# Second conv matrix ahead of the pool matrix, with seven block products for eight in half of its columns

## The chip, the cores and the metric

The kernel runs on one core of a Trainium2 chip. TensorE (PE) does the matrix products, VectorE (DVE) and ScalarE (ACT) work on vectors, GpSimd (POOL) and SyncE (SP) here mostly issue transfers from the chip's memory (HBM). Each engine works through its own queue of instructions in order and waits on semaphores for the others. The metric is the time of one execution on the device in microseconds (us), lower is better.

## The reference

One layer of a hybrid decoder in 32-bit floats: 256 tokens behind 16 learned ones, width 2048. What matters here is the middle of it:

```python
proj = u @ w_in[l]
z_pool, v_conv, g_conv, gate_a, gate_b = jnp.split(proj, splits, axis=-1)
y_a = causal_multiscale_pool(z_pool, w_pool_grp[l], pool_scale[l]) @ w_pool_out[l]
y_b = conformer_conv(v_conv, g_conv, w_dw[l], b_dw[l],
                     conv_ln_g[l], conv_ln_b[l]) @ w_conv_out[l]
m = jax.nn.sigmoid(gate_a) * y_a + jax.nn.sigmoid(gate_b) * y_b
h = h + rms_norm(m @ w_o[l], g_post_mix[l])
```

`conformer_conv` ends in a LayerNorm over 1024 channels and a swish; the result, here called s_act (256 x 1024), goes through the second conv matrix w_conv_out (1024 x 2048). The pooled branch is a small matrix per group of channels (w_pool_grp), then w_pool_out (1024 x 2048). An up and a down matrix of width 8192 follow behind w_o.

## The kernel before

**Split numbers.** Every matrix product is made from three: each 32-bit operand is split into a high part (a cast to the format that PE multiplies at full rate) and a low part (what is left), and PE adds high x high, high x low and low x high. Weights come in chunks of 1 MB, 128 x 2048 floats on chip. SP loads a chunk into one of three raw buffers, ACT casts the high part (line 276), DVE subtracts to get the low part (line 279), PE multiplies. High and low parts have three slots each, so the cast of chunk n waits until PE has done with chunk n - 3, and a raw buffer comes free when its low part is made.

**Order.** The order of each queue is written out by the program (`tc.manual_schedule()`). A list `stream` (lines 206 to 233) names the chunks in the order of their use; `fetch` (line 296) opens and splits the chunks up to two ahead of the one that it hands to PE, and then flushes the list `late` of waiting ACT work. `project_t` (line 844) is the loop of the stages here: per chunk a fetch, then 12 matmuls for each of two halves of 128 tokens (line 839), each 128x512 out; after the last chunk of a block of 512 columns, an evacuation. A list `pending` holds the small steps of the pooling and of the conv branch; `drain` issues them between blocks of matmuls, as many as a credit of microseconds (`fill`) allows, and a FETCH entry lets the rest wait for the next fetch. The LayerNorm's steps are such items: sums by PE (cs_m, cs_v), a root on ACT, a reciprocal chain on DVE (L448 to L452, `ln_newton`), the normalising product (L809), 16 activations on ACT in a row (`affine`, L814 and L815), the swish product (L820), and the split of s_act (L823, L826). Later parts of the kernel (the w_o, up and down matrices) use `Plan` (line 23), which takes work items with an engine, a cost, what they read and write, and sets their order: PE's and SP's items as written, DVE's and ACT's by when they can begin and when they are due.

**The stages around the change.** Eight gate projections of 2048 x 512 columns (b = 0: gate_a, b = 1: gate_b; `acc_gate`, four chunks each; a sigmoid into `sg[b]`), the pooled groups (`acc_grp`, one chunk w_grp, 48 matmuls of 128x256, L493), the pool matrix (`acc_po`, four blocks of two chunks; L904 multiplies the result by the gate in place), the conv matrix (`acc_co`, likewise; L953 multiplies by the second gate, L954 adds the two branches, and PE transposes the merged block, `mt`), and w_o (`o_c` and others). When the conv matrix begins, POOL's queue starts `early_sums` (line 918): four loads of 1 MB, two of them adding onto what is there, into the room of an activation that is then free. Rooms are shared by tag: "um" and "ux" hold u, the input of the gates, and after it m and `pairs_room`.

**Seven for eight.** The w_o, up and down stages already multiply in blocks by Strassen's way: a 2 x 2 block product with seven products of sums of blocks in place of eight. `sums_of_m` (line 967) makes four such sums of the activations:

```python
a11, a12, a21, a22 = (A[:, t, h] for t in range(2) for h in range(2))
nc.vector.tensor_sub(a11, a11, a21)
nc.vector.tensor_sub(a21, a21, a22)
nc.vector.scalar_tensor_tensor(a22, a11, -1.0, a22, op0=ALU.mult, op1=ALU.subtract)
nc.vector.tensor_add(a12, a12, a22)
```

## Time and profile before

| | |
|---|---|
| median of three runs | 1184.01 us (1183.78, 1184.01, 1185.14) |
| the profiled execution | 1184.03 us, span 1182.3 us |
| gates, last one ends | 327.85 us |
| pooled groups | 327.85 to 333.60 us |
| pool matrix | 333.60 to 377.15 us |
| conv matrix, with transposes | 377.15 to 423.37 us |
| mean granted TensorE clock | 0.998 of full speed |

Times in the trace count from the start of the span. In a row such as `L279 DVE TENSOR_TENSOR lo<-raw,hi 128x2048 ... x16 | 36.6, 2290 | 22.8 <-ACT hi` the line and engine come first, then what is written from what, how often, busy us and mean ns of one, then the engine's idle time just before these instructions and what ended it. In a timeline row the first number is the start, the second the duration. In the rows of the stretches each engine's busy us are followed by its count of instructions, then the granted clock, the busy share of the DMA engines and GB/s.

### The profile page before, as it was taken

The numbers are of one execution on the slowest core, as the hardware profiler recorded it, in microseconds if no ns is written. First come the engines' busy times: TensorE is split into PE (matmuls) and PEld (weight loads), VectorE is DVE, ScalarE is ACT, GpSimd is POOL, SyncE is SP. The second block draws the span as 40 slices with busy tenths as digits, with TensorE's granted clock in tenths as the row PEclk, the third lists the DMA queues.
The fourth block names the chain that finished last, engine by engine and source line by source line (L and its number), as shares of the span: only waits on it lengthen the run. The fifth ranks groups of instructions, "written<-read, shape, count | busy, mean of one in ns | idle before, by whom it ended". The sixth has DMA issues, their size and how long they took to land.

```text
span 1182.3 us, 15772 instructions
## 1 busy us (share of the span) xinstructions
PE 1172.6 (99%) x6351; PEld 1019.5 (86%) x6351; DVE 1012.0 (86%) x1095; ACT 679.9 (58%) x690; POOL 45.0 (4%) x51
## 2 busy tenths in 40 slices
PE   9999999999999999999999999999999999999997
PEld 9999988888888888898888888888888888888886
DVE  6899989986665799988998988989989989889865
ACT  6543344445754466756566766666756667666642
POOL 1000000000000001000001001000000010010000
PEclk9999999999999999999999999999999999999999
DMA  8655565555566967859869899898998998998861
GB/s 295 213 179 179 181 199 190 192 200 181 181 209 227 271 214 219 288 167 323 242 220 241 233 292 231 233 291 226 282 293 213 274 275 228 281 240 239 303 215 72
DMA packets 177883, 272.91 MB, mean 231 GB/s; under 512 B 4658, under 2 KB 92914, under 8 KB 176913
## 3 DMA queue, kind: packets, MB, share of 16 engines
q1 hardware_dynamic: 160176, 235.88, 59.2%
q0 software_dynamic: 16736, 34.76, 16.1%
q10 hardware_dynamic: 896, 1.25, 0.3%
q8 instruction: 50, 0.82, 0.3%
q14 instruction: 25, 0.20, 0.0%
HBM read 267.68 MB, written 4.19 MB: 230 GB/s over the span
## 4 chain that ended last, share of the span: by engine, by line
PE 99%; DVE 0%; DVEq 0%; issue 0%; ACT 0%; ACTq 0%
PE bank_u L498 18%; PE acc_gate L839 15%; PE bank_a L1802 10%; PE bank_u L504 9%; PE acc_up L1802 8%; PE bank_b L1802 7%; PE o_c L1185 6%; PE acc_z L493 4%; PE acc_co L839 4%; PE acc_po L839 4%; PE acc_v L493 3%; PE acc_g L493 3%; PE acc_vg L493 2%; PE acc_up L498 1%; PE bank_u L1802 1%; PE o_b L1185 1%
## 5 line engine op out<-in xcount | busy, mean ns | idle before, releaser
L498 PE MATMUL bank_u<-m,hi 128*128 128x512 f32 x960 | 328.8, 389 | 0.0
L504 PE MATMUL bank_u<-m,lo 128*128 128x256 f32 x960 | 265.2, 276 | 0.0
L276 ACT CAST hi<-raw 128x2048 fp32r<-128x2048 f32 (+2 forms) x94 | 151.1, 1620 | 187.8 <-PE acc_gate L839 37.6
L279 DVE TENSOR_TENSOR lo<-raw,hi 128x2048 fp32r<-128x2048 f32 (+2 forms) x94 | 179.8, 1924 | 60.4 <-ACT hi L276 60.1
L498 PEld LDWEIGHTS bank_u<-m,hi 128*128 128x128 f32 x960 | 180.2, 188 | 37.7
L1585 DVE TENSOR_TENSOR lo<-raw_m,hi 128x2048 fp32r<-128x2048 f32 x70 | 160.2, 2288 | 31.2 <-ACT hi L1581 31.1
L504 PEld LDWEIGHTS bank_u<-m,lo 128*128 128x128 f32 x960 | 180.2, 188 | 1.4
L1581 ACT CAST hi<-raw_m 128x2048 fp32r<-128x2048 f32 x70 | 133.9, 1913 | 74.5 <-DVE raw_m L1598 21.3
L839 PE MATMUL acc_gate<-hi,u_um 128*128 128x512 f32 x416 | 131.0, 389 | 0.0
L559 DVE SCALAR_TENSOR_TENSOR c<-a,taps,c 128x256 f32<-128x256 f32 x240 | 98.3, 473 | 0.1
L1802 PE MATMUL bank_a<-hi,forms 128*128 128x512 f32 (+1 forms) x288 | 93.5, 386 | 0.0
L839 PEld LDWEIGHTS acc_gate<-hi,u_um 128*128 128x128 f32 x416 | 78.1, 188 | 16.1
L839 PE MATMUL acc_gate<-lo,u_um 128*128 128x512 f32 x208 | 80.9, 389 | 0.0
L1585 DVE TENSOR_TENSOR lo<-raw_a,hi 128x2048 fp32r<-128x2048 f32 x29 | 66.3, 2287 | 10.8 <-ACT hi L1581 10.7
L1581 ACT CAST hi<-raw_a 128x2048 fp32r<-128x2048 f32 x29 | 55.4, 1910 | 33.8 <-PE bank_u L498 12.3
L1581 ACT CAST hi<-raw_c 128x2048 fp32r<-128x2048 f32 x27 | 51.5, 1909 | 27.2 <-PE bank_u L498 12.2
L1585 DVE TENSOR_TENSOR lo<-raw_c,hi 128x2048 fp32r<-128x2048 f32 x27 | 61.7, 2287 | 5.7 <-ACT hi L1581 5.7
L1802 PEld LDWEIGHTS bank_a<-hi,forms 128*128 128x128 f32 x288 | 53.9, 188 | 11.0
L1585 DVE TENSOR_TENSOR fourth_pair<-raw_m,fourth_pair 128x2048 fp32r<-128x2048 f32 x26 | 59.4, 2286 | 4.4 <-ACT fourth_pair L1581 4.4
L1665 ACT COPY half<-bank_u 128x256 f32<-128x256 f32 x60 | 22.2, 370 | 65.6 <-PE bank_u L504 65.6
L1802 PE MATMUL acc_up<-hi,forms 128*128 128x512 f32 x176 | 57.5, 390 | 0.0
L1802 PE MATMUL bank_a<-lo,forms 128*128 128x512 f32 (+1 forms) x144 | 55.6, 386 | 0.0
(419 smaller groups left out, 2266.9 us busy)
## 6 DMA issues: line engine op xcount, KB each, us to landing
raw<-in_w_in_dram SPq DMA_DIRECT2D x52, 1024.0 KB, 5.0
raw_m<-in_w_down_dram SPq DMA_DIRECT2D x38, 1024.0 KB, 7.1
raw_m<-in_w_down_dram POOLq DMA_DIRECT2D x22, 1024.0 KB, 10.5
raw_a<-in_w_up_dram SPq DMA_DIRECT2D x20, 1024.0 KB, 6.5
raw_c<-in_w_up_dram SPq DMA_DIRECT2D x19, 1024.0 KB, 6.4
raw_m<-in_w_up_dram SPq DMA_DIRECT2D x19, 1024.0 KB, 6.7
raw_a<-in_w_down_dram SPq DMA_DIRECT2D x13, 1024.0 KB, 7.3
raw_c<-in_w_down_dram SPq DMA_DIRECT2D x13, 1024.0 KB, 7.4
```

The lines of the kernel that those rows point to most:

```text
L276: nc.scalar.copy(hi[:, sl, cs], raw[:, sl, cs])
L279: nc.vector.tensor_sub(lo[:, sl, cs], raw[:, sl, cs], f32(hi[:, sl, cs]))
L493: nc.tensor.matmul(acc, w[:, k[0], cs], act[:, k[1], a, off:], start=first and n == 0, stop=last and n == 2)
L498: nc.tensor.matmul(acc.rearrange("p (a t) -> p a t", a=2)[:, :, ts], hi[:, k[0], cs], act[:, k[1], :, off + ts.start:off + ts.stop], start ...
L504: nc.tensor.matmul(acc[:, :T], lo[:, k[0], cs], act[:, k[1], 0, off:], start=False, stop=stop, skip_group_check=True)
L559: nc.vector.scalar_tensor_tensor(c, conv["a"][:, q, i:i + T], taps[:, q, i:i + 1], c, op0=ALU.mult, op1=ALU.add)
L839: nc.tensor.matmul(acc, act(kk)[:, a_, ts_], w_[:, k, :], start=kk == 0 and n == 0, stop=kk == nk - 1 and n == 2)
L1185: nc.tensor.matmul(acc, form(k, a_), box[w_][:, k, :], start=start and k == 0 and n == 0, stop=stop and k == CK - 1 and n == 2, skip_group ...
L1581: nc.scalar.copy(box["hi"], raw)
L1585: nc.vector.tensor_sub(box["lo"], raw, f32(box["hi"]))
L1665: nc.scalar.copy(box[j], accs[j][:, :T])
L1802: nc.tensor.matmul(acc, forms[h][:, f, k, a_, :], box[w_][:, k, cs], start=start and k == 0 and n == 0, stop=stop and k == KH - 1 and n == ...
```

## The change

The pool and the conv matrix change places: the conv matrix is now multiplied straight after the last gate, and the pool matrix comes behind it. For that the LayerNorm's steps are issued one to three chunks earlier, and the pooled groups stand ahead of the last gate, so that their chunk w_grp is ahead of the last gate's four chunks.

The conv matrix has 4 x 2 blocks of weights (512 columns by half of the 1024 channels). Column blocks 2 and 3 are multiplied as before (X20, X21, X30, X31, each for the two halves a and b of the tokens: 8 products of 12 matmuls). Column blocks 0 and 1, with two halves of channels and two halves of tokens, are made from seven products (named 1 to 7, in the order 1 5 2 6 7 3 4) in place of eight. Their four weight blocks are loaded once, into the room of u ("um"), and four of the seven operands are sums made there on DVE, in place, 128x2048 each; all operands are split as chunks are. Four sums of s_act's blocks (`conv_sums`) and their splits (`conv_forms`) are made as well. Products share three PSUM banks; ACT copies a bank to `pairs` where a partial sum is wanted later (`keep`), and DVE joins them (`joined`). The conv stage's work is given to a `Plan`, with the splits of the first two chunks of the pool matrix in it. Each finished block is multiplied by its gate in place (`gate_conv`, eight products of 128x512), and the merge of the two branches moves to the pool matrix (`evac_merged`).

Three places of the queues show it. The first is ACT's queue at the LayerNorm's 16 activations (`sq` and `c`). Before, the two casts ahead and the one behind are of chunks of the last two gates (`hi_2905` is the third chunk of the last gate):

```order
L276 CAST hi_2825<-raw_2824 128x2048
L276 CAST hi_2857<-raw_2856 128x2048
L814 ACTIVATE sq<-c,vecs 128x256
L815 ACTIVATE c<-c,vecs 128x256
...
L815 ACTIVATE c<-c,vecs 128x256
L276 CAST hi_2905<-raw_2904 128x2048
L868 ACTIVATE sg_2459<-acc_gate_0_2745,r_in 128x512
L868 ACTIVATE sg_2459<-acc_gate_1_2746,r_in 128x512
L276 CAST hi_2939<-raw_2938 128x2048
```

Now:

```order
L283 CAST hi_2760<-raw_2759 128x2048
L283 CAST hi_2797<-raw_2796 128x2048
L821 ACTIVATE sq<-c,vecs 128x256
L822 ACTIVATE c<-c,vecs 128x256
...
L822 ACTIVATE c<-c,vecs 128x256
L283 CAST hi_2845<-raw_2844 128x2048
L283 CAST hi_2875<-raw_2874 128x2048
L877 ACTIVATE sg_2459<-acc_gate_0_2757,r_in 128x512
L877 ACTIVATE sg_2459<-acc_gate_1_2758,r_in 128x512
L283 CAST hi_2908<-raw_2907 128x2048
```

The cast behind the activations (`hi_2845`) is now that of the pooled groups' weights, which PE uses ahead of the last gate.

The second is DVE's queue at the border between the two matrices. Before, `lo_3310` is the low part of the first chunk of the conv matrix, and the products around it write the gated pool blocks:

```order
L904 TENSOR_TENSOR sg_1856<-acc_po_0_3242,sg_1856 128x512
L904 TENSOR_TENSOR sg_1856<-acc_po_1_3243,sg_1856 128x512
L279 TENSOR_TENSOR lo_3310<-raw_3308,hi_3309 128x2048
L279 TENSOR_TENSOR lo_3340<-raw_3338,hi_3339 128x2048
L904 TENSOR_TENSOR sg_1856<-acc_po_0_3306,sg_1856 128x512
L904 TENSOR_TENSOR sg_1856<-acc_po_1_3307,sg_1856 128x512
L279 TENSOR_TENSOR lo_3384<-raw_3382,hi_3383 128x2048
L279 TENSOR_TENSOR lo_3414<-raw_3412,hi_3413 128x2048
L953 TENSOR_TENSOR mts<-acc_co_0_3380,sg_2459 128x512
L954 TENSOR_TENSOR mts<-mts,sg_1856 128x512
```

Now, at the end of the conv stage, with `lo_3347` the low part of the last product's weights, `lo_3385` and `lo_3389` those of the pool matrix's first two chunks:

```order
L1009 TENSOR_TENSOR lo_3347<-conv_blocks,hi_3343 128x2048
L1040 TENSOR_TENSOR sg_2459<-pairs,sg_2459 128x512
L1040 TENSOR_TENSOR sg_2459<-acc_ca_3134,sg_2459 128x512
L1040 TENSOR_TENSOR sg_2459<-acc_cb_3151,sg_2459 128x512
L1040 TENSOR_TENSOR sg_2459<-acc_ca_3196,sg_2459 128x512
L1040 TENSOR_TENSOR sg_2459<-acc_cb_3214,sg_2459 128x512
L1045 TENSOR_TENSOR pairs<-pairs 128x512
L1040 TENSOR_TENSOR sg_2459<-pairs,sg_2459 128x512
L1009 TENSOR_TENSOR lo_3385<-raw_c_3209,hi_3361 128x2048
L1045 TENSOR_TENSOR pairs<-acc_co_3128,pairs 128x512
L1040 TENSOR_TENSOR sg_2459<-pairs,sg_2459 128x512
L1009 TENSOR_TENSOR lo_3389<-raw_c_3229,hi_3367 128x2048
```

The first low part of the following matrix stood right behind a product on the block two before; it now stands behind a join, five gate products, another join and its gate product.

The third is SP's queue. Before, one load of a chunk after another:

```order
L271 DMA raw_3244<-in_w_pool_out_dram 128x4x512
L271 DMA raw_3274<-in_w_pool_out_dram 128x4x512
L271 DMA raw_3308<-in_w_conv_out_dram 128x4x512
L271 DMA raw_3338<-in_w_conv_out_dram 128x4x512
L271 DMA raw_3382<-in_w_conv_out_dram 128x4x512
L271 DMA raw_3412<-in_w_conv_out_dram 128x4x512
L271 DMA raw_3448<-in_w_conv_out_dram 128x4x512
L271 DMA raw_3494<-in_w_conv_out_dram 128x4x512
```

Now, from the first chunk of the conv matrix on:

```order
L278 DMA raw_3052<-in_w_conv_out_dram 128x4x512
L278 DMA raw_3091<-in_w_conv_out_dram 128x4x512
L981 DMA raw_c_3129<-in_w_conv_out_dram 128x4x512
L981 DMA raw_c_3131<-in_w_conv_out_dram 128x4x512
L985 DMA conv_blocks<-in_w_conv_out_dram 128x4x512 x4
L981 DMA raw_c_3209<-in_w_pool_out_dram 128x4x512
L981 DMA raw_c_3229<-in_w_pool_out_dram 128x4x512
L278 DMA raw_3402<-in_w_pool_out_dram 128x4x512
```

The four loads into `conv_blocks` stand in a row, and the loads of the pool matrix's first chunks (`raw_c_3209`, `raw_c_3229`, `raw_3402`) are queued behind them.

The diff, cut to its core:

```diff
+        if n == 2 * D // CW - 1:
+            stream.append((w_grp.rearrange("g (k p) c -> p (g k) c", p=P), (NG * GD // P, GD)))
         stream += columns(w_in, 0, KD, G0 + n * CW)
-    stream.append((w_grp.rearrange("g (k p) c -> p (g k) c", p=P), (NG * GD // P, GD)))
-    for w, nk in ((w_pool_out, KP), (w_conv_out, KC)):
-        for n in range(NB):
-            stream += columns(w, 0, nk, n * CW)
+
+    def conv_block(kb, n):
+        return columns(w_conv_out, kb * CK, CK, n * CW)[0]
+
+    UNITS = "X20a X20b X21a X21b X30a X30b 1 5 2 6 X31a X31b 7 3 4".split()
+    CONV = list(dict.fromkeys(u_.rstrip("ab") for u_ in UNITS))
+    stream += [conv_block(int(key[2]), int(key[1])) for key in CONV[:2]]
+    for n in range(NB):
+        stream += columns(w_pool_out, 0, KP, n * CW)
...
-    def project_t(act, nk, evac, name, fill=0.0):
+    def project_t(act, nk, evac, name, fill=0.0, often=False):
...
+                if often and t:
+                    flush()
...
-    for b in range(2):
-        sg[b] = big.tile([P, NT, D], F32, tag=f"s{b}", name=f"sg{b}")
-        for n in range(NB):
-            project_t(u_of, KD, evac_gate(b, n), f"gate{b}{n}", fill=2.9)
-
-
-    y = big.tile([P, KP, 2, T], F32R, tag="k8", bufs=2, name="y")
-    hi, lo = fetch()
-    for g in range(NG):
-        for j in range(GK):
-            q = g * GK + j
-            acc = (acc_tile if q < KP - 2 else misc_tile)(f"acc_grp_{q}")[:, :T]
-            for k in range(GK):
-                mm3(acc, hi, lo, d, (g * GK + k, g * GK + k), slice(j * P, (j + 1) * P),
-                    k == 0, k == GK - 1)
-            nc.scalar.activation(y[:, q, 0, :], acc, AF.Copy, scale=col("pool_scale", q))
-            nc.vector.scalar_tensor_tensor(y[:, q, 1, :], acc, col("pool_scale", q),
-                                           f32(y[:, q, 0, :]), op0=ALU.mult, op1=ALU.subtract)
-    drain(2.0)
...
-        pending[0:0] = [FETCH, a_[2], b_[2]]
-    pending += [(0, ln_out), (0, ln_act)]
...
-    def evac_pool(n):
-        def f(t, acc):
-            nc.vector.tensor_mul(sg[0][:, t, block(n)], acc, sg[0][:, t, block(n)])
-        return f
+        pending[0:0] = [FETCH, a_[2], b_[2], (2.4, conv_sums), FETCH] + [
+            (0.6, conv_low(key)) for key in "56"]
+    FORM_C = {"5": (0, (1, 0)), "6": (1, (1, 1)), "7": (0, (0, 0)), "3": (1, (0, 1))}
+    Sc = []
+
+    def conv_a(t, h):
+        return conv["c"][:, h * CK:(h + 1) * CK, t * P:(t + 1) * P]
+
+    def conv_sums():
+        a11, a12, a21, a22 = (conv_a(t, h) for t in range(2) for h in range(2))
+        nc.vector.tensor_sub(a11, a11, a21)
+        nc.vector.tensor_sub(a21, a21, a22)
+        nc.vector.scalar_tensor_tensor(a22, a11, -1.0, a22, op0=ALU.mult, op1=ALU.subtract)
+        nc.vector.tensor_add(a12, a12, a22)
+        Sc.append(big.tile([P, 2, CK, 2, P], F32R, tag="a", name="conv_forms"))
+        late.extend(conv_high(key) for key in "56")
+
+    def conv_high(key):
+        f, at_ = FORM_C[key]
+        return lambda: nc.scalar.copy(Sc[0][:, f, :, 0, :], conv_a(*at_))
+
+    def conv_low(key):
+        f, at_ = FORM_C[key]
+        return lambda: nc.vector.tensor_sub(Sc[0][:, f, :, 1, :], conv_a(*at_),
+                                            f32(Sc[0][:, f, :, 0, :]))
+
+    def pooled_groups():
...
+    for b in range(2):
+        sg[b] = big.tile([P, NT, D], F32, tag=f"s{b}", name=f"sg{b}")
+        for n in range(NB):
+            if (b, n) == (1, NB - 1):
+                y = pooled_groups()
+                pending += [(0, ln_out), (0, ln_act)]
+            project_t(u_of, KD, evac_gate(b, n), f"gate{b}{n}", fill=2.9, often=b)
...
-        project_t(y_of, KP, evac_pool(n), f"po{n}", fill=2.4)
...
+    blocks_room = big.tile([P, 4, CK * CW], F32, tag="um", name="conv_blocks")
+    ROOM_C = {"1": 0, "5": 0, "6": 0, "4": 0, "7": 1, "3": 2, "2": 3}
+    BLOCK_C = ((0, 0), (0, 1), (1, 1), (1, 0))
+    SUM_C = {"5": (0, 1), "6": (0, 2), "4": (0, 3), "7": (1, 2)}
+    conv_banks = {"ch": misc_tile("acc_co_chain"), "w2": misc_tile("acc_co_2"),
+                  "w3": acc_tile("acc_co_3")}
+    BANK_C = {"1": "ch", "6": "ch", "7": "ch", "4": "ch", "2": "w2", "5": "w3", "3": "w3"}
...
+    def load_block(i):
+        cplan.add("SP", 3.1, lambda: nc.sync.dma_start(
+            blocks_room[:, i].rearrange("p (k c) -> p k c", k=CK), conv_block(*BLOCK_C[i])[0]),
+            writes=(f"block{i}",), late=3.0)
...
+        name = f"block{ROOM_C[key]}" if key in ROOM_C else of_load[e]
+        if key in SUM_C:
+            to, more = SUM_C[key]
+            cplan.add("DVE", 2.22, lambda: nc.vector.tensor_add(
+                blocks_room[:, to], blocks_room[:, to], blocks_room[:, more]),
+                reads=(f"block{more}",), writes=(f"block{to}",))
+
+        def high():
+            box["hi"] = part_tile("hi", n)
+            nc.scalar.copy(box["hi"], room())
+
+        def low():
+            box["lo"] = part_tile("lo", n)
+            nc.vector.tensor_sub(box["lo"], room(), f32(box["hi"]))
+            conv_parts[e] = tuple(box[h].rearrange("p (k c) -> p k c", k=CK) for h in HALVES)
+        cplan.add("ACT", 1.83, high, reads=(name,), writes=(f"hi{q}",))
+        cplan.add("DVE", 2.22, low, reads=(name, f"hi{q}"), writes=(f"lo{q}",))
...
+    def keep(n, t, bank):
+        cplan.add("ACT", 0.5, lambda: nc.scalar.copy(h_room(n, t), conv_banks[bank]),
+                  reads=(bank,), writes=(h_of(n, t),))
+
+    def gate_conv(n, t, bank=None):
+        cplan.add("DVE", 0.62, lambda: nc.vector.tensor_mul(
+            sg[1][:, t, block(n)], conv_banks[bank] if bank else h_room(n, t),
+            sg[1][:, t, block(n)]), reads=(bank or h_of(n, t),))
+
+    def joined(n, t, op, a_, b_, names):
+        cplan.add("DVE", 0.62, lambda: op(h_room(n, t), a_(), b_()), reads=names,
+                  writes=(h_of(n, t),))
+        gate_conv(n, t)
...
+    load_c(*wanted_c.pop(0), ahead=True)
+    load_c(*wanted_c.pop(0), ahead=True)
+    for i in range(4):
+        load_block(i)
+    load_c(*wanted_c.pop(0))
+    split_done = 2
+    begun_c = set()
+    for u_, unit in enumerate(UNITS):
+        e = entry_of[unit.rstrip("ab")]
+        while split_done < len(CONV) + 2 and used.get(split_done - 3, -1) < u_ and split_done <= e + 3:
+            split_c(split_done, CONV[split_done] if split_done < len(CONV) else "pool")
+            if split_done in of_load and wanted_c:
+                load_c(*wanted_c.pop(0))
+            split_done += 1
...
+            for k in range(CK):
+                for n, (a_, w_) in enumerate(((0, hi), (0, lo), (1, hi))):
+                    nc.tensor.matmul(conv_banks[bank], form(k, a_), w_[:, k, :],
+                                     start=start and k == 0 and n == 0,
+                                     stop=k == CK - 1 and n == 2, skip_group_check=True)
+        q = slot_c(e)
+        cplan.add("PE", 2.72, product, reads=[f"hi{q}", f"lo{q}"] + (
+            [f"S{FORM_C[unit][0]}"] if unit in FORM_C else []), writes=(bank,))
+        if unit == "1":
+            keep(0, 0, "ch")
+        elif unit == "5":
+            keep(0, 1, "w3")
+            form_parts("7")
+        elif unit == "6":
+            keep(1, 0, "ch")
+            form_parts("3")
+        elif unit == "2":
+            joined(0, 0, nc.vector.tensor_add, lambda: conv_banks["w2"], lambda: h_room(0, 0),
+                   ("w2", h_of(0, 0)))
+        elif unit == "7":
+            keep(1, 1, "ch")
+            joined(1, 1, nc.vector.tensor_sub, lambda: h_room(0, 1), lambda: h_room(1, 1),
+                   (h_of(0, 1), h_of(1, 1)))
+        elif unit == "3":
+            joined(1, 0, nc.vector.tensor_sub, lambda: conv_banks["w3"], lambda: h_room(1, 0),
+                   ("w3", h_of(1, 0)))
+        elif unit == "4":
+            gate_conv(0, 1, "ch")
+        elif kb:
+            gate_conv(int(unit[1]), "ab".index(unit[3]), bank)
...
+    cplan.emit()
+    for e in ahead_p:
+        opened.append((*conv_parts[e], [], flats[e]))
...
-    def evac_conv(n):
+    def evac_merged(n):
         def f(t, acc):
             mt = mt_of(n, t)
-            nc.vector.tensor_mul(mt, acc, sg[1][:, t, block(n)])
-            nc.vector.tensor_add(mt, mt, sg[0][:, t, block(n)])
+            nc.vector.tensor_mul(mt, acc, sg[0][:, t, block(n)])
+            nc.vector.tensor_add(mt, mt, sg[1][:, t, block(n)])
...
-        project_t(s_act_of, KC, evac_conv(n), f"co{n}")
+        project_t(y_of, KP, evac_merged(n), f"po{n}")
```

More of the change, by code (lines that the diff above doesn't have):

```diff
@@ L918, in hybrid_block @@
+    while split_done < len(CONV) + 2:
+        split_c(split_done, "pool")
+        split_done += 1
+    assert not wanted_c
+    cplan.emit()
+    for e in ahead_p:
+        opened.append((*conv_parts[e], [], flats[e]))
+    at["parts"] = first_c + len(CONV) + 2
+    at["n"] += 2
     early_sums = big.tile([P, 2, CK * CW], F32, tag="k8", bufs=2, name="early_sums")
@@ L1037, in hybrid_block @@
     plan = Plan()
-    HALVES = ("hi", "lo")
     SA1, SA2, SA3, SA4 = ((1, 0), (1, 1), (0, 0), (0, 1))
```

79 lines of the change are left out of this document (75 added, 4 removed).

## The prediction

> **What bounds the kernel now.** I read the page's first part and the list of waits, then the chain of waits around the change, then busy time by stage.
>
> ```profile
> PE 1172.6 (99%) x6351; PEld 1019.5 (86%) x6351; DVE 1012.0 (86%) x1095; ACT 679.9 (58%) x690; POOL 45.0 (4%) x51
> PE idle L394 <- DVE rb L308: 1.1, 1, 1.1
> 289.50 0.24 PE cs_v L480 x2
> 289.74 38.11 PE acc_gate L839 x168
> 327.85 5.75 PE acc_grp L493 x48
> 333.60 43.55 PE acc_po L839 x192
> 377.15 16.33 PE acc_co L839 x72
> ...
> 423.37 2.73 PE o_c L1185 x12
> core 0: us, PE busy (x) PEld busy (x) DVE busy (x) ACT busy (x) POOL busy (x), PEclk, DMA share, GB/s
> 333.50:377.00 43.50, 43.50 (x194) 36.01 (x194) 26.65 (x22) 19.05 (x14) 0.00 (x0) 1.00 0.57 192
> 377.00:423.20 46.20, 46.20 (x217) 38.53 (x216) 33.55 (x32) 20.58 (x18) 4.16 (x4) 1.00 0.83 251
> ```
>
> PE waits once in the whole run, for 1.1 us, and in all stages that the change touches it is the chain: gates to 327.85, pooled groups to 333.60, pool matrix to 377.15, conv matrix to 423.37. So a matmul that is taken away is a gain, and any wait that appears on PE is a full loss. A 128x512 matmul costs 43.55 / 192 = 0.2268 us, a block of 24 (one chunk of weights) 5.44 us, a product of 12 2.72 us. DVE has room on average: 26.65 of 43.5 us in the pool stage, 33.55 of 46.2 in the conv stage. The question is whether that room stands where the new DVE work falls.
>
> The prices of the work that feeds PE, from the same two stages:
>
> ```profile
> L279 DVE TENSOR_TENSOR lo<-raw,hi 128x2048 fp32r<-128x2048 f32 x16 | 36.6, 2290 | 22.8 <-ACT hi L276 22.8
> L276 ACT CAST hi<-raw 128x2048 fp32r<-128x2048 f32 x16 | 30.6, 1914 | 32.5 <-PE acc_po L839 24.5 <-PE acc_co L839 7.1 <-DMA raw<-in_w_conv_out_dram 0.9
> 341.05 2.29 DVE L279 TENSOR_TENSOR lo<-raw,hi 128x2048 fp32r<-128x2048 f32 x1 [2.81 <-ACT hi L276]
> 343.26 0.68 DVE L904 TENSOR_TENSOR sg<-acc_po,sg 128x512 f32<-128x512 f32 x1
> 343.86 1.22 DVE L826 TENSOR_TENSOR s_act<-c,s_act 128x1024 fp32r<-128x1024 f32 x1
> 377.19 1.91 ACT L276 CAST hi<-raw 128x2048 fp32r<-128x2048 f32 x1 [2.01 <-PE acc_po L839]
> 379.13 2.29 DVE L279 TENSOR_TENSOR lo<-raw,hi 128x2048 fp32r<-128x2048 f32 x1 [1.25 <-ACT hi L276]
> ```
>
> Back to back on DVE a 128x2048 operation advances the queue by 343.26 - 341.05 = 2.21 us, a 128x512 one by 0.60. The high part starts 0.04 us after the PE block that frees its slot (377.15 to 377.19), the low part 1.94 us after that.
>
> **The change, part by part.** *Products.* Columns 0 and 1 of the conv matrix take seven products in place of eight: 192 - 180 = 12 matmuls fewer, -2.72 us. That is all the change can gain, 0.23% of the run; against it stand waits.
>
> *Order of the LayerNorm.* The conv matrix needs s_act first, so its chain runs one to three chunks earlier. The two matmuls of cs_v stand two chunks earlier on PE, behind a DVE subtraction that had slack of a chunk; I take 0.2 us of waiting (0 to 0.5).
>
> ```profile
> 293.73 1.75 DVE L448 RECIPROCAL ln_r<-ln_q 128x256 f32<-128x256 f32 x1
> 297.24 2.29 DVE L279 TENSOR_TENSOR lo<-raw,hi 128x2048 fp32r<-128x2048 f32 x1
> 299.45 2.35 DVE L809 TENSOR_TENSOR c<-c,ln_r 128x1024 f32<-128x1024 f32 x2
> 285.96 1.26 ACT L868 ACTIVATE sg<-acc_gate,r_in 128x512 f32<-128x512 f32 x2
> 302.55 0.59 ACT L814 ACTIVATE sq<-c,vecs 128x256 f32<-128x256 f32 x1
> ...
> 311.57 1.89 ACT L276 CAST hi<-raw 128x2048 fp32r<-128x2048 f32 x1
> 313.49 2.29 DVE L279 TENSOR_TENSOR lo<-raw,hi 128x2048 fp32r<-128x2048 f32 x1 [8.53 <-ACT hi L276]
> ```
>
> *The block of 16 LayerNorm activations.* It holds ACT for 311.57 - 302.55 = 9.02 us, and a weight cast stands behind it. Before, that cast ends in a low part at 313.49 + 2.29 = 315.78, while PE wants it about 316.97 + 0.23 (327.85 less two blocks, plus a matmul): 1.4 us to spare. After, the cast behind it is that of the pooled groups. Its time, on the old clock: the block boundary at 284.06 (327.85 less eight blocks and cs_v's 0.24), two sigmoids first (1.26), the cast from 285.24, its low part from 287.18 to 289.39, the reciprocal chain (297.24 - 293.73 = 3.51) to 292.90, half of the normalising product to 294.2, the activations to 303.22, the cast of the pooled groups' weights, their low part from 305.16 to 307.45. PE wants it after the seventh gate at 327.85 - 21.78 = 306.07, at its third matmul, 0.24 later, and 0.1 to 0.2 more for the wait at cs_v. The wait is about 1.1 us (0.5 to 1.6). What is queued behind on ACT is the next cast, which has a block of slack.
>
> *The conv stage on DVE.* Let T0 be its first matmul. Part slots are three, so the cast for product "1" starts when the second column block ends: T0 + 5.44 + 0.04, its low part at T0 + 7.42. From there to the end of the low part of the first pool chunk the DVE queue holds 9 low parts, the 4 weight sums and 10 operations of 128x512 (two forms, two joins, six gate products): 13 x 2.21 + 10 x 0.60 = 34.7. To that come some 0.5 for operations that read the result just ahead of them and some 0.8 for waits on products not yet ended: 36.1, so T0 + 43.5. PE ends its fifteen products at T0 + 40.8 and wants that low part one matmul later, at T0 + 41.03: a wait of 2.5 us. The least is 34.7 without any wait, 1.1 us; the most I put at 3.5, twice the extras. Before, a conv or pool chunk's low part stands two chunks ahead of its use; here six gate products and two joins, whose results no one wants soon, stand ahead of it. Inside the stage the other low parts are in time by my walk, product "2" with 0.5 us, "5" with 2.3; the last product may wait 0.3 for a copy on ACT, which shortens the later wait by as much. ACT casts 11 chunks where it cast 8 and copies four banks: some 25 us of 41, hidden.
>
> *Four weight blocks.* They load into u's room, which PE frees nine matmuls (2.0 us) ahead of T0, so with a short issue about T0 - 1.9. The nearest rows are the burst that ends in the up matrix:
>
> ```profile
> 521.52 0.37 SPq L271 DMA_DIRECT2D raw<-in_w_up_dram  x1
> ...
> 524.94 5.22 SPq L1537 DMA_DIRECT2D raw_m<-in_w_down_dram  x2
> raw<-in_w_up_dram SPq DMA_DIRECT2D x1, 1024.0 KB, 6.1
> ...
> raw_m<-in_w_down_dram SPq DMA_DIRECT2D x1, 1024.0 KB, 11.7
> ```
>
> Four loads issued from 521.52 to 524.94 land from 527.6 to 536.6: the first after 6.1 us, the others 3.0 apart. So the blocks land at T0 + 4.2, 7.2, 10.2, 13.2. They are wanted at 5.5, 9.9, 12.3 and 16.5: nothing, with 1.3 to 3.3 us of cover. If that cover goes, the whole DVE queue shifts.
>
> *The pool stage's loads.* A raw buffer comes free with its low part, so a late first chunk makes the loads late. Let P be the stage's first matmul. The raw loads for its fourth to sixth chunk are issued at about P + 2.5, P + 6 and P + 8.8; before, the loads of the last stage were issued one per block, at 370.6, 376.0 and 381.4 against its start at 377.15 (first line below: four from 376.01 on), so 9.0, 7.1 and 4.5 us earlier. The four early_sums loads on POOL's queue start at P as they did before, two of them accumulating.
>
> ```profile
> 376.01 16.69 SPq L271 DMA_DIRECT2D raw<-in_w_conv_out_dram  x4
> raw<-in_w_in_dram SPq DMA_DIRECT2D x52, 1024.0 KB, 5.0
> raw<-in_w_conv_out_dram SPq DMA_DIRECT2D x4, 1024.0 KB, 10.9
> early_sums<-in_w_o_dram POOLq DMA_DIRECT2D x4, 1024.0 KB, 11.7
> raw<-in_w_conv_out_dram SPq DMA_DIRECT2D x1, 1024.0 KB, 8.3
> q1 hardware_dynamic: 528, 1.05, 39.3%
> 400.40 1.92 ACT L276 CAST hi<-raw 128x2048 fp32r<-128x2048 f32 x1 [0.88 <-DMA raw<-in_w_conv_out_dram]
> ```
>
> The next four lines are issues with median time to landing: 5.0 us commonly, 10.9 beside early_sums, 8.3 for the load that starts just into them. The sixth line is SP's queue (q1) from 394 to 402, while the sums accumulate: 1.05 MB in 8 us. The last shows that a cast already waited for such a load. So the three land at P + 10.8, + 18.8 and + 26.8 by these rows, a microsecond later if the first shares more; cast and low part of the sixth chunk then end at P + 31.1 to 32.6 with little queued ahead, and PE wants it at 2.5 + 0.2 + 5 x 5.44 + 2 x 0.87 (two groups of transposes) = P + 31.6. I take 0.8 us (0 to 2.5). [...]
>
> *The rest.* Eight gate products move from the pool stage into the conv stage and the final merge has the two operations it had; counted above or unchanged. The w_o weights that wait for the gates' room come one DVE operation (0.7 us) later, against about 1 us of slack there: nothing.
>
> Sum: -2.72 + 0.2 + 1.1 + 2.5 + 0.8 = +1.9 us. The profiled execution took 1184.03 us (span 1182.3), the median is 1184.01, so the sum goes on the median: 1185.9.
>
> **Rivals.**
> (a) *DVE keeps up in the conv stage; not slower.* The first pool chunk's low part is ready by T0 + 41.0. For that DVE must do its 36.1 us of queue in 33.6, or start 2.5 earlier. For it: PE and ACT were never late here before. Against it: 34.7 us is bare work at back-to-back prices, and the slot rule sets the start. Sum 1183.4.
> (b) *No wait anywhere.* Then 1184.0 - 2.7 = 1181.3. It needs (a) and a LayerNorm chain more than a microsecond quicker.
> (c) *Loads late.* The four blocks share the queues' time and land together near T0 + 13, as 11.7 us for the last suggests; product "1" then starts over 7 us late, or the pool stage's loads each land one block later than I took: 1188 to 1193. Against it: loads in the burst landed in order, 3 us apart.
> (d) *The clock falls in the longest wait.* The granted clock is 1.00 in every row above and no wait of PE exceeds 1.1 us, so nothing shows what a wait of 2.5 us does; if 3.4 us of matmuls ran at half clock after it, 1.7 us more: 1187.6. [...]
>
> **How the numbers follow.** Forecast as summed, terms between their bounds (1184.8 to 1188): 0.57. (a) 0.14, (b) 0.06, (c) 0.15, (d) 0.08. About 0.2% (2.4 us) is what a measurement of this kernel can tell from no change; the lines are 1181.6 and 1186.4. Faster is (b), 0.06. Same is (a) and half of the forecast's own, 0.42. Slower is the rest, 0.52. The range leaves out (b) and the upper part of (c): 1182.8 to 1189.8.
>
> **What would show it.** Waits of PE for DVE's low part: at the pooled groups about 1 us, at the second matmul of the pool matrix 2 to 2.5, and a smaller one late in the pool stage, with a DMA behind its cast. DVE near full from T0 + 7.4 to T0 + 43.5. Blocks landing 3 us apart. If PE's waits in the conv stage itself are above 1 us, my walk of that stage is wrong; if DVE sits idle there for ACT or DMA, the loads or casts were mispriced.

## The result, and the profile after

The changed kernel takes 1189.9 us in the median of six runs (1189.2 to 1191.0) against 1183.9 before: 1.0049 of the time, 95% interval 1.0036 to 1.0062. It is slower by 6.0 us. Its profiled execution took 1189.37 us with a span of 1187.7, 5.4 us more than the profiled one of before; the shares below add up to these 5.4.

The page's first part:

```profile
PE 1173.8 (99%) x6339; PEld 1018.4 (86%) x6339; DVE 1034.4 (87%) x1113; ACT 690.0 (58%) x701; POOL 45.0 (4%) x51
```

The list of PE's waits (us in total, times, longest), which had one entry before:

```profile
PE acc_po L846 <- DVE lo L1009: 2.1, 1, 2.1
PE idle L401 <- DVE rb L315: 1.1, 1, 1.1
PE acc_grp L500 <- DVE lo L286: 0.9, 1, 0.9
PE mt L1140 <- ACT m L1144: 0.7, 1, 0.7
PE mt L1140 <- DVE mts L1159: 0.3, 1, 0.3
PE acc_co_chain L1086 <- ACT pairs L1036: 0.2, 1, 0.2
```

Four waits are new that cost more than a matmul each, and with the small one on ACT they come to 4.2 us. But PE has also become busier, 1173.8 us against 1172.6, with 12 matmuls less. Matmuls must have taken longer somewhere. The chain of waits of the changed kernel gives the stages (start and length in us):

```profile
278.69 0.44 PE cs_v L487 x2
...
303.19 1.91 ACT hi L283
305.12 2.30 DVE lo L286
307.46 5.76 PE acc_grp L500 x46
...
335.01 2.72 PE acc_ca L1086 x12
```

The conv stage begins at 335.01, where the pool stage began at 333.60 before: 1.41 later. Of that 0.07 stand already at the start of the rows (269.85 for 269.78), 0.20 in the row of cs_v, and the other 1.14 at the pooled groups, where the chain runs through the cast at 303.19 and its low part. The lengths of the two matrix stages come from PE's timeline, where a row starts some 0.16 us ahead of the chain's:

```profile
334.85 0.39 PE L1086 MATMUL acc_ca<-hi,s_act 128*128 128x512 f32 x1
...
373.25 0.50 PE L1086 MATMUL acc_co_chain<-hi,s_act 128*128 128x512 f32 x1 [0.15 <-ACT pairs L1036]
...
376.10 0.39 PE L846 MATMUL acc_po<-hi,y 128*128 128x512 f32 x1
...
428.06 0.39 PE L1385 MATMUL o_c<-hi,m 128*128 128x512 f32 x1
```

The conv stage takes 41.25 us (334.85 to 376.10) for 180 matmuls of 40.82: 0.43 lost, all at the last product, which waits for a copy on ACT. The pool stage takes 51.96 us (376.10 to 428.06); the corresponding stage before took 423.37 - 377.15 = 46.22. So the pool stage alone lost 5.74 us. Busy time by stretch, in columns as before, shows that the clock was not at full speed all through:

```profile
375.60:379.01 3.41, 1.35 (x6) 0.80 (x6) 3.41 (x3) 1.90 (x1) 1.56 (x2) 1.00 0.27 22
379.01:382.43 3.42, 3.42 (x10) 2.64 (x9) 3.38 (x4) 0.00 (x0) 0.00 (x0) 0.50 0.91 369
```

PE's timeline behind the first matmul of the pool matrix:

```profile
378.55 0.50 PE L846 MATMUL acc_po<-lo,y 128*128 128x512 f32 x1 [2.06 <-DVE lo L1009]
...
379.62 0.63 PE L846 MATMUL acc_po<-lo,y 128*128 128x512 f32 x1
380.05 1.05 PE L846 MATMUL acc_po<-hi,y 128*128 128x512 f32 x2
...
383.00 0.39 PE L846 MATMUL acc_po<-lo,y 128*128 128x512 f32 x1
```

The second matmul of the pool matrix starts 2.45 us after the first, where 0.23 would do: 2.22 lost. Behind it the starts lie up to 0.43 apart, twice the usual distance, until 382.5; the granted clock is 0.50 from 379.01 to 382.43. From 378.55 to 383.00 are 12 matmuls, 2.72 us at full speed: 1.73 lost to the slow clock. On DVE's timeline the low part that PE waits for stands behind the gate products:

```profile
371.89 0.69 DVE L1040 TENSOR_TENSOR sg<-pairs,sg 128x512 f32<-128x512 f32 x1
...
376.21 2.28 DVE L1009 TENSOR_TENSOR lo<-raw_c,hi 128x2048 fp32r<-128x2048 f32 x1
```

The remaining 1.8 us of the pool stage (5.74 - 2.22 - 1.73) lie almost all at two of its three groups of transposes. The raw loads issued at 378.6, 382.0 and 384.9 with their time to landing:

```profile
raw<-in_w_pool_out_dram SPq DMA_DIRECT2D x1, 1024.0 KB, 9.2
raw<-in_w_pool_out_dram SPq DMA_DIRECT2D x1, 1024.0 KB, 12.6
raw<-in_w_pool_out_dram SPq DMA_DIRECT2D x1, 1024.0 KB, 17.8
```

and the chain of waits from the last of them:

```profile
384.85 17.83 DMA raw<-in_w_pool_out_dram
402.76 1.92 ACT hi L283
404.70 2.29 DVE lo L286
406.99 0.61 DVE mts L1158
```

A load that takes 17.8 us makes a late cast and a late low part. The low part itself is in time for PE, but behind it on DVE stands the merge of a finished block (L1158, L1159), and PE's transposes need that merge. Beyond the pool stage w_o runs as before; between 537 and 560 us, in the up matrix, another 0.6 us goes, without a wait that the profile names. Executions of the kernel before's own up matrix show the same 0.6 (below), so it is not shown to be the change's.

### The profile page after: what moved, and what is told of

Its sections match the earlier page's. It is cut to its first block, busy times and chain, and to the rows that moved or that the text cites. A ratio compares the mean times of both kernels' runs of the same rounds, so it can differ in the third digit from the quotient of the medians.

```text
span 1187.7 us, 15784 instructions
## 1 busy us (share of the span) xinstructions
PE 1173.8 (99%) x6339; PEld 1018.4 (86%) x6339; DVE 1034.4 (87%) x1113; ACT 690.0 (58%) x701; POOL 45.0 (4%) x51
## 4 chain that ended last, share of the span: by engine, by line
PE 93%; DVE 3%; DMA 2%; ACT 1%; issue 1%; DVEq 0%; ACTq 0%
PE bank_u L505 18%; PE acc_gate L846 13%; PE bank_a L2002 10%; PE bank_u L511 9%; PE acc_up L2002 8%; PE bank_b L2002 7%; PE o_c L1385 6%; PE acc_z L500 4%; PE acc_v L500 3%; PE acc_g L500 3%; PE acc_vg L500 2%; DMA raw<-in_w_pool_out_dram 2%; PE acc_up L505 1%; DVE lo L286 1%; PE bank_u L2002 1%; PE acc_ca L1086 1%
## 5 line engine op out<-in xcount | busy, mean ns | idle before, releaser
L283 ACT CAST hi<-raw 128x2048 fp32r<-128x2048 f32 (+2 forms) x86 | 135.5, 1591 | 157.0 <-PE acc_gate L846 31.7
L286 DVE TENSOR_TENSOR lo<-raw,hi 128x2048 fp32r<-128x2048 f32 (+2 forms) x86 | 161.6, 1891 | 38.3 <-ACT hi L283 38.1
L1785 DVE TENSOR_TENSOR lo<-raw_a,hi 128x2048 fp32r<-128x2048 f32 x29 | 66.3, 2287 | 10.8 <-ACT hi L1781 10.7
L1781 ACT CAST hi<-raw_c 128x2048 fp32r<-128x2048 f32 x27 | 51.5, 1908 | 26.8 <-PE bank_u L505 12.4
```

The costliest lines, as they stand in the source:

```text
L283: nc.scalar.copy(hi[:, sl, cs], raw[:, sl, cs])
L286: nc.vector.tensor_sub(lo[:, sl, cs], raw[:, sl, cs], f32(hi[:, sl, cs]))
L1781: nc.scalar.copy(box["hi"], raw)
L1785: nc.vector.tensor_sub(box["lo"], raw, f32(box["hi"]))
```

## The experiments

The kernel before, run again beside these versions, took 1184.2 to 1184.4 us in the median. The text set off in each case is what was expected before that run.

**Gate products behind the pool matrix's first low parts.**

```diff
-        cplan.add("DVE", 0.62, lambda: nc.vector.tensor_mul(
...
+        if wait:
+            gates_c.append(gate)
+        else:
+            cplan.add("DVE", 0.62, gate, reads=(bank or h_of(n, t),))
...
     cplan.emit()
+    for gate in gates_c:
+        gate()
```

> The changed kernel with six of the eight gate products of the conv stage taken out of its planned DVE order and issued behind the low parts of the pool matrix's first two chunks; nothing else moves. Theory A (order of the DVE queue): the gate products ahead of the first low part make the 2.06 us wait at the pool matrix, the wait makes the slow clock behind it (about 1.7 us more), and the lateness makes the waits at the transposes (about 1.5): all three go, 5 to 5.5 us, so about 1184.5. Theory B (amount of DVE work): the wait only moves to the third or fourth chunk of the pool matrix, 1187 to 1189. Theory C (contention with early_sums makes the waits at the transposes, whatever DVE's order): the first two go, 3.9 us, and the waits at the transposes stay, about 1186.

The edit moves seven of the eight, all but the one that ACT's copy waits for; five of them had stood ahead of the first pool low part. Measured: 1186.45 us (1184.5 to 1189.2 in eleven runs), ratio 1.0022 (1.0013 to 1.0031); 3.4 us less than the changed kernel. PE's waits in its profiled execution:

```profile
PE mt L1149 <- DVE mts L1168: 1.7, 2, 1.0
...
PE mt L1149 <- ACT m L1153: 0.7, 1, 0.7
```

and a cast on ACT's timeline:

```profile
388.78 1.91 ACT L283 CAST hi<-raw 128x2048 fp32r<-128x2048 f32 x1 [5.50 <-DMA raw<-in_w_pool_out_dram]
```

The wait for the first low part is gone, and with it the slow clock (the granted clock is 1.00 from 375.7 to 383). That is theory A's first half. Its second half falls: the waits at the transposes stay and are even longer, 2.4 us by the list, and ACT waits for the raw loads. Theory C holds for them. The pool stage now takes 425.28 - 375.88 = 49.4 us, still 3.2 too many.

**early_sums held until the first pool block is merged.**

```diff
-    early_sums = big.tile([P, 2, CK * CW], F32, tag="k8", bufs=2, name="early_sums")
...
         project_t(y_of, KP, evac_merged(n), f"po{n}")
+        if n == 0:
+            early_sums = big.tile([P, 2, CK * CW], F32, tag="k8", bufs=2, name="early_sums")
+            for e in range(2):
+                nc.vector.tensor_copy(early_sums[:, e, :1], mt_of(n, 1)[:, :1])
...
```

> The changed kernel with the four early_sums loads held until the first block of the pool matrix is merged, some 13 us later. Theory A: the wait at the pool matrix (2.06 us) and the slow clock stay as they are; the raw loads of that stage land in 5 to 8 us in place of 9 to 18, and the waits at the transposes (1.0 us by the list of waits) go with their tails: 1188.3 to 1188.9. Theory C: contention is most of the pool stage's loss, 1186 or less. Rival: the held loads meet later chunks or w_o instead and nothing is won, 1189.5 to 1191.

Measured: 1185.61 us, ratio 1.0018 (1.0009 to 1.0027); 4.3 us less than the changed kernel, as much as theory C asked for (1186 or less). The four loads now begin at 391.5 in place of 376.9. In the list of waits the one at the pool matrix is unchanged, those at the transposes are gone:

```profile
PE acc_po L846 <- DVE lo L1009: 2.1, 1, 2.1
```

The raw loads of the pool stage, with the median time to landing:

```profile
raw<-in_w_pool_out_dram SPq DMA_DIRECT2D x5, 1024.0 KB, 6.4
```

and busy time around the wait, which begins ahead of 377.29 and ends at 378.13:

```profile
373.88:377.29 3.41, 2.19 (x10) 1.49 (x8) 3.38 (x5) 2.16 (x2) 0.00 (x0) 1.00 0.00 0
377.29:380.70 3.41, 2.57 (x11) 2.12 (x12) 3.38 (x4) 0.54 (x1) 0.00 (x0) 1.00 0.44 94
```

The raw loads land in 6.4 us in the median, so the waits at the transposes come of the contention with early_sums. The held loads now meet the first two loads of w_o's weights, which take 12.6 us in the median in place of 6.0; PE doesn't wait for those. And behind the same wait of 2.06 us, as long as in the changed kernel, the clock here stays at 1.00: the fall is not certain. So theory C's time comes in part of the clock, and contention is not most of the loss. The pool stage takes 424.33 - 375.69 = 48.64 us by PE's timeline, 3.3 less than in the changed kernel: 1.7 of that is the slow clock that did not come, and 1.6, of 5.7 lost in all, the transposes. Its eleven runs make two groups, seven from 1185.1 to 1185.7 with a mean clock of 0.998 and four from 1187.3 to 1187.7 with 0.996 or 0.997. The distance is about that of one slow stretch. That the upper group is the executions in which the clock fell is what the mean clocks suggest; rows exist only of one execution, from the lower group.

**LayerNorm activations one chunk later.**

```diff
-            late.append(affine)
+            affines.append(affine)
...
     for step in range(2):
         pending += [FETCH] + [half[step] for half in ln_halves]
+        if not step:
+            pending += [LATER] * 2 + [(0, lambda: late.extend(affines))]
```

> The changed kernel with the 16 LayerNorm activations issued one chunk later on ACT, so that the cast of the pooled groups' weights stands ahead of them and the first cast of the last gate behind. If the activations ahead of that cast make the wait at the pooled groups, it goes: PE's wait of 0.9 us and its tail, 1.1 us in all, about 1188.8, with the rest of the run as it was. Rival: the cast behind is late in its turn, or the swish product and the split of s_act come too late for the conv stage, and the time stays at 1189.9 or rises.

Measured: 1192.26 us, ratio 1.0067 (1.0054 to 1.0079), 2.4 us more than the changed kernel. The rival holds: the cast behind is late in its turn. The rows of ACT, DVE and PE around PE's new wait on the timeline:

```profile
305.83 1.89 ACT L283 CAST hi<-raw 128x2048 fp32r<-128x2048 f32 x1
...
312.92 3.22 DVE L929 SCALAR_TENSOR_TENSOR y<-acc_grp,vecs,y 128x256 fp32r<-128x256 f32 x8
313.46 0.50 PE L849 MATMUL acc_gate<-hi,u_um 128*128 128x512 f32 x1 [1.88 <-DVE y L929]
```

The wait at the pooled groups is gone. But the casts of the last gate now stand behind the activations, their low parts are late on DVE, and behind these stand the evacuations of the pooled groups' banks (y), which the last gate needs free: 1.9 us, 0.8 more than was won. In this execution a wait at the transposes of 2.4 us was followed by a fall of the clock, too, while the wait of 2.1 us at the pool matrix was not.

**The exchange alone, with eight products.**

```diff
-    stream += [conv_block(int(key[2]), int(key[1])) for key in CONV[:2]]
+    for n in range(NB):
+        stream += columns(w_conv_out, 0, KC, n * CW)
...
-    cplan = Plan()
...
+    for n in range(NB):
+        project_t(s_act_of, KC, evac_first(n), f"co{n}")
```

> The changed kernel's order (LayerNorm early, conv matrix ahead of the pool matrix, gate product in place, merge in the pool stage) with eight products in all columns, multiplied in the plain loop: no weight sums, no forms, no joins. By my sum the reordering costs the wait at the pooled groups (1.1 us) and at the LayerNorm's second sum (0.2), nothing in either matrix stage: 1185.3. Rival: the reordering costs more by itself, because the pool stage then meets early_sums with another rhythm: 1186.5 to 1188. If it is 1184, the waits ahead of the conv stage cost nothing on the whole.

Measured: 1185.09 us, ratio 1.0006 (0.9997 to 1.0015), where 1185.3 was expected. Its only new wait in the list:

```profile
PE acc_grp L501 <- DVE lo L287: 0.9, 1, 0.9
```

Both matrix stages run without one. So the pool stage's loss does not come with the order of the matrices; it comes with the seven products' work on DVE. That the exchange costs 0.9 us is inside the interval of no change.

**Both edits in the pool stage** (the first two diffs together).

> The changed kernel with both edits, the six gate products behind the first two pool low parts and early_sums held until the first pool block is merged. If the DVE order and the contention are two causes that add, no wait of PE is left in the pool stage: 1189.9 less 2.2 (wait), 1.7 (slow clock) and 1.6 to 2.0 (waits at the transposes and their tails), so 1183.5 to 1184.5, and the runs no longer fall into two groups 2 us apart as those with only early_sums held did (1185.1 to 1185.7 and 1187.3 to 1187.7). If the gate products only move the lateness on, a wait at the transposes stays: 1185.5 to 1187.

Measured: 1183.6 us, ratio 0.9998 (0.9989 to 1.0007). Beside 1.1 us and 0.5 us (for an input) at the start only one wait of PE is in the list, and none in the pool stage:

```profile
PE acc_grp L500 <- DVE lo L286: 0.9, 1, 0.9
```

The two causes add up: 6.3 us less than the changed kernel, and the pool stage takes 46.3 us, as the last stage did before. Nine of eleven runs lie between 1183.1 and 1184.6, but two lie at 1185.3 and 1185.9, and no rows exist of those.

**A third edit, the activations on either side of the cast.**

```diff
-            late.append(affine)
+            (affines if q0 else late).append(affine)
...
+            pending += [LATER] * 2 + [(0, lambda: late.extend(affines))]
...
     def pooled_groups():
-        hi, lo = fetch()
+        hi, lo = fetch(ahead=1)
```

> The same with a third edit: eight of the 16 LayerNorm activations ahead of the cast of the pooled groups' weights and eight behind it, and the second chunk of the last gate split after the pooled groups' evacuations and not ahead of them. That edit of all 16 at once had only moved the wait to the last gate, whose banks then waited for the evacuations on DVE. If the wait at the pooled groups is this order alone, its 1.1 us go: 1182.0 to 1183.2, below the kernel before. If a wait stays at the last gate's first or second chunk, 1183.5 to 1184.5.

Measured: 1182.45 us, ratio 0.9986 (0.9977 to 0.9994): faster than the kernel before by 1.9 us and than the changed one by 7.4. PE waits nowhere but for the 1.1 us at the start; busy time in the stretch of the pooled groups and the last gate, and in the pool stage:

```profile
305.30:332.80 27.50, 27.50 (x146) 23.74 (x145) 22.86 (x23) 18.03 (x21) 0.00 (x0) 1.00 0.62 209
...
373.60:420.40 46.80, 46.80 (x220) 38.98 (x219) 39.23 (x42) 20.70 (x19) 4.16 (x4) 1.00 0.88 270
```

**The exchange alone with the third edit.**

> The kernel with the exchanged order and eight products in all columns, with the third edit of the run before (eight of the 16 LayerNorm activations on either side of the cast of the pooled groups' weights, the second chunk of the last gate split later). If the order of ACT's queue is all that the exchange costs, its wait at the pooled groups goes and the time is that of the kernel before plus the 0.2 us at cs_v: 1184.0 to 1184.6. Then the seven products are worth the rest of the way to the version with all three edits (1182.45), 1.5 to 2.2 us of the 2.72 that their matmuls are. If the exchange costs something else too, 1185 or more, as without the edit (1185.09).

Measured: 1184.06 us, ratio 0.9999 (0.9990 to 1.0008), 1.0 us less than without the edit. The exchange costs nothing that can be measured once ACT's order is mended. Beside the version with all three edits this makes the seven products worth about 1.6 us of the 2.72 that their matmuls are (the kernel before had 1184.43 beside the one and 1184.37 beside the other); the two intervals leave more than a microsecond either way. In the chain's rows of the two executions the conv stage takes 43.52 us with eight products and 41.26 with seven, 2.3 less. The 0.43 at the copy on ACT is what is missing there from 2.72.

**The clock behind a wait, measured by itself.** The kernel before, with the low parts of two chunks of the pool stage written several times over; the longer probe has (4, 0) and (4, 2) in place of (2, 6) and (3, 3):

```diff
             nc.vector.tensor_sub(lo[:, sl, cs], raw[:, sl, cs], f32(hi[:, sl, cs]))
+            full, part = {60: (2, 6), 64: (3, 3)}.get(n, (0, 0))
+            for i in range(full):
+                nc.vector.tensor_sub(lo[:, sl, cs], raw[:, sl, cs], f32(hi[:, sl, cs]))
+            for i in range(part):
+                nc.vector.tensor_sub(lo[:, 0, cs], raw[:, 0, cs], f32(hi[:, 0, cs]))
```

> The kernel before with the low parts of two chunks of the pool stage computed several times over (the same result written again), so that PE waits for DVE about 1.2 us at the fourth and 1.6 us at the eighth chunk of that stage. If waits of this length leave the clock alone: 1184.0 + 2.8 = 1186.8 in all runs. If a wait above about 1 us can halve the clock behind it: 1.7 us more for each, in some runs or in all, 1188.5 to 1190.

> The same with about 2.0 and 3.2 us of waiting. Without an effect on the clock 1184.0 + 5.2 = 1189.2. If the clock falls as it did behind the 2.06 us wait in the changed kernel, 1.7 us more per wait: 1191 to 1192.6, with the granted clock of the stretch behind the wait near 0.77. If the fall depends on how the wait lies in a window that runs on its own, the runs spread over both.

Measured: 1190.93 us (1190.2 to 1191.3) and 1193.97 (1193.4 to 1194.1). The waits came out longer than planned. In the shorter probe they add 4.6 us and one fall of the clock 1.7: 1190.7. The profiled execution of the longer one also waited 1.4 us for an input at its start. PE's rows on the timeline at the two waits of the shorter probe:

```profile
352.26 0.50 PE L844 MATMUL acc_po<-lo,y 128*128 128x512 f32 x1 [2.24 <-DVE lo L284]
376.93 0.50 PE L844 MATMUL acc_po<-lo,y 128*128 128x512 f32 x1 [2.38 <-DVE lo L284]
```

The same rows of the longer one:

```profile
353.60 0.50 PE L844 MATMUL acc_po<-lo,y 128*128 128x512 f32 x1 [2.53 <-DVE lo L282]
379.87 0.80 PE L844 MATMUL acc_po<-lo,y 128*128 128x512 f32 x1 [3.98 <-DVE lo L284]
```

Within one execution a wait of 2.24 us left the clock alone and one of 2.38 us halved it, a few matmuls after PE had begun again, for 3.4 us; one of 2.53 left it alone, one of 3.98 halved it. The runs do not spread as widely as two independent falls would make them. The wait's length alone does not decide between 2.1 and 2.5 us.

Its place does, as far as these executions show. In the changed kernel and in both probes the stretch of half clock behind a wait lasts 3.41 us, and in the changed kernel the changes of the clock lie a whole number of such lengths apart: it falls at 379.01 and again at 1181.15, when PE has nothing left to do, 235 lengths later. So each execution can be cut into windows of 3.41 us, counted from a change of the clock. The rows show the window that holds most of each wait of the shorter probe, with the fall behind the second, and then the fall in the longer one:

```profile
350.63:354.04 3.41, 1.78 (x8) 1.46 (x9) 3.34 (x6) 1.10 (x1) 0.00 (x0) 1.00 0.19 23
...
374.53:377.94 3.41, 1.02 (x5) 0.86 (x5) 3.31 (x6) 3.21 (x3) 0.00 (x0) 1.00 0.00 0
377.94:381.35 3.41, 3.41 (x9) 2.67 (x8) 3.41 (x3) 0.00 (x0) 0.00 (x0) 0.50 0.93 305
```

```profile
376.09:379.50 3.41, 0.00 (x0) 0.00 (x0) 3.34 (x3) 2.99 (x3) 0.00 (x0) 1.00 0.00 0
379.50:382.91 3.41, 3.04 (x7) 2.47 (x8) 3.41 (x4) 0.00 (x0) 0.00 (x0) 0.50 0.52 153
```

With early_sums held, counted back from the fall at the end of that execution (1179.42), the 2.06 us wait lies over two windows, and the clock stays; in the changed kernel it lay in one, the window from 375.60, with PE busy for 1.35 us of 3.41 (the rows of both stand above).

In the rows here and above, and at the end of the changed kernel's execution (PE busy for 1.42 us from 1177.74 to 1181.15, the clock at 0.50 behind), every window in which PE was busy for 42% or less was followed by a window at half clock, and no window with 52% or more was; none lies between. This was read off afterwards, and no run was made to test it. In the two executions with a wait of 2.06 us the windows lay differently against the wait, and it came out either way.

## Why the prediction was right or wrong

The forecast was slower, by 1.9 us, and the change is slower, by 6.0; the ratio times 1184.0 is 1189.8, the upper end of the range. That it still lies inside is luck: the forecast's own bounds ended at 1188, and the range went on to 1189.8 for a part of rival (c), whose late blocks and loads a block later did not come. What filled that room was rival (d)'s slow clock and a term that was set too small. Term by term, against the profiled execution:

| step of the prediction | forecast, us | measured, us |
|---|---|---|
| 12 matmuls fewer | -2.72 | -2.73 |
| cs_v earlier | +0.2 | +0.20 |
| pooled groups behind the activations | +1.1 | +1.14 |
| first pool low part behind the gate products | +2.5 | 2.22, and 0.43 ahead at the copy on ACT |
| slow clock behind that wait | 0, rival (d) | +1.73 |
| pool stage's loads beside early_sums | +0.8 | about +1.8 |
| beyond the pool stage | 0 | +0.6, not shown to be the change's |
| sum (with 0.07 at the start and -0.05 in w_o) | +1.9 | +5.4 |

**Right.** The product count, the two waits ahead of the conv stage, and the walk along DVE's queue: forecast 2.5 us with 0.3 of it possibly at the copy on ACT, measured 2.22 and 0.43. The low part ended at T0 + 43.5 by the sum, and 376.21 + 2.28 - 335.01 = 43.48 in the trace. The edit that moved the gate products took the wait away, so it is their order. The four weight blocks landed as the burst had shown, the first 5.4 us after its issue and the others 2.7 apart, and no wait came of them; neither half of rival (c) happened.

**Wrong by a rival judged too unlikely.** Rival (d) had 0.08 and its price was right, 1.7 forecast and 1.73 measured. No row in the prediction shows the 3.4 us at half clock that this price rests on; the changed kernel's row shows 3.42 us at 0.50. I had taken 2.5 us for too short a wait, which no run had shown. The measurement decides: 2.06 us of waiting were followed by half the clock, as was every window of 3.41 us shown above in which PE was busy for 42% or less. That the same wait of 2.06 us left the clock alone with early_sums held fits how it lay: over two such windows there, in one in the changed kernel.

**Wrong in a term's size.** "The pool stage's loads" were forecast to land at P + 10.8, 18.8 and 26.8, and they landed at P + 11.7, 18.5 and 26.6. The arrival was right; what was wrong is the step from it, "cast and low part of the sixth chunk then end at P + 31.1 to 32.6 with little queued ahead, and PE wants it at P + 31.6". That low part ended at P + 30.9 and PE didn't wait for it. I had asked what stands ahead of it on DVE and not what stands behind: the merge of the second block, which the transposes wait for. It cost some 1.8 us where I had 0.8. The range of that term, 0 to 2.5, held it. Slow loads alone do not make this wait: in the kernel before the load of the last stage's sixth chunk, too, ran into early_sums and took 8.3 us, but it was issued 4.3 us behind the stage's first matmul and not 8.8, and PE never waited.

**Open.** The 0.6 us in the up matrix. From w_o to the 12 products at the head of the up matrix's second part (`bank_a`) it is 131.1 us in the kernel before, in the exchange alone and with the gate products moved, and 131.7 in the changed kernel and in the versions with two and three edits. But it is 131.7 also in the exchange alone with the third edit and in both probes, whose up matrix is the kernel before's. The row of `bank_a` in the kernel before, whose w_o begins at 423.37, and both rows of the shorter probe:

```profile
554.48 2.75 PE bank_a L1802 x12
```

```profile
430.29 2.73 PE o_c L1190 x12
561.99 2.78 PE bank_a L1807 x12
```

So it comes without the change too, and may be chance in the one profiled execution of the changed kernel. No wait is listed in either, and no run tells what it hangs on.

Rival (a), that DVE keeps up, fell with its own argument: the slot rule set the start and 34.7 us of bare work followed. Rival (b) is what three edits come near to: 1181.3 by its sum, 1182.45 measured.

## What to carry to other kernels

Where a planner orders an engine's queue by when work can begin, work that no one waits for fills the place ahead of work that becomes possible a moment later; at the last stage of a plan, let such work stand behind the first inputs of the next stage. A late operand can cost more than its wait (here 1.73 us of slow clock came behind 2.06 of waiting): ask for what is queued behind it on its engine, for the loads that its buffer sets free, and for the clock. And beside four transfers in the background, two of which add onto memory, the weights' loads took 9.2 to 17.8 us here, where the 52 loads of w_in took 5.0 in the median; so start such transfers when the loads ahead have their lead, not at the stage's border.

## What the runs showed of the hardware

The TensorE clock halved for 3.41 us behind waits of 2.06, 2.38, 2.4 and 3.98 us and stayed at full speed behind others of 2.06, 2.1, 2.24 and 2.53 us; behind the 0.9 us at the pooled groups it was 1.00. The fall in the changed kernel cost 1.73 us, beside a wait of 2.06. What told the two apart in the windows shown was how busy PE had been in the 3.41 us ahead: for at most 1.42 us (42%) where the clock fell, for at least 1.78 us (52%) where it did not.

The second is how far contention reaches: beside the four early_sums loads a 1 MB load took 9.2, 12.6 and 17.8 us in one row of three, and 6.4 in the median when those loads started some 15 us later. Less moved while the two of them that add onto memory were in flight: in the kernel before, with the two plain ones (first row) and with the two adding ones (second row), the DMA engines were as busy (1.03 and 1.10), but moved 394 and 262 GB/s:

```profile
379.00:385.00 6.00, 6.00 (x28) 4.96 (x27) 2.72 (x2) 2.01 (x2) 0.02 (x1) 1.00 1.03 394
394.00:402.00 8.00, 8.00 (x39) 6.66 (x38) 3.83 (x4) 5.61 (x6) 0.00 (x0) 1.00 1.10 262
```
